# A fourth PSUM bank for the attention scores, and the epilogue's transposes in the bank of the product with the values

## The chip, the core and the metric

The kernel runs on one NeuronCore of one Trainium2 chip. The metric is device time of one execution in microseconds (us), as the median of several executions. The engines are named as the profile names them: PE is TensorE (PEld are its weight loads), DVE is VectorE, ACT is ScalarE, POOL is GpSimd, and SP is SyncE, which issues the DMAs. A line such as L1026 is a line of the kernel before.

## What is computed

One decoder layer over 2048 tokens of width 1024. After an RMSNorm and one input projection, half of the width goes through a gated DeltaNet (a chunked linear attention with a recurrent state), and the other half through a differential attention; an output projection brings both back to the residual stream. The change touches the differential attention, of which the core is:

```python
def block(args):                      # 128 queries against all earlier keys, 4 heads, 2 maps each
    q_blk, start = args
    s = jnp.einsum('bqhcd,bkhcd->bhcqk', q_blk, k).astype(jnp.float32)
    mask = key_pos[None, :] <= (start + jnp.arange(Q_BLOCK))[:, None]
    p = jax.nn.softmax(jnp.where(mask, s, neg), axis=-1)
    wts = p[:, :, 0] - lam * p[:, :, 1]
    return jnp.einsum('bhqk,bkhv->bqhv', wts.astype(v.dtype), v)
...
o = rmsnorm(o, out_gain) * (1.0 - lambda_init)
o = o * jax.nn.silu(z)                # then concatenated, and x + mixed @ w_out
```

## The kernel before, in words

Up to 1119 us of the profiled execution the kernel does the input projections and the DeltaNet. What follows is the attention, with the output projection mixed in between.

The attention works on 32 groups of 256 queries, in the order of the table SEQ: first the lower half of the sequence for the four heads (sixteen groups, with 2 to 8 blocks of 128 keys), then the upper half (sixteen groups, with 10 to 16 blocks). For each half group (qt is 0 or 1, 128 queries) three streams run side by side (`abreast`):

- `scores` (L1000): for each 512 keys and each of the two maps, PE writes a tile `sp` into a PSUM bank (two matmuls of 512 columns, and on the diagonal a third with the mask `cmask`), DVE takes the maximum `nm` (L1024), and ACT the exponential `ex` (L1026). The bank is free for a later tile when `ex` has ended.
- `values` (L1056) of the half group before: DVE joins the two maps (L1078), PE transposes the result into a bank `wtp`, ACT or DVE copies it to `wt`, and in the second half group PE accumulates `wt` times the values into one bank, `oT` (2g+2 products; each stands in the trace as two matmuls).
- `epilogue` (L1113) of the group before: ACT copies `oT` to `ob` (L1117), PE transposes it into `onp`, DVE clips it (`cl`, L1124), ACT squares it with a sum, DVE and POOL work out the norm (`aok`, `aso`, `afo`), DVE scales (`aon`, L1138), PE transposes it back into `aotp`, and DVE multiplies with the gate (`azz`, L847). ACT and POOL then split the result into two parts (`mxh`, `mxl`).

Beside these runs `behind`: the output projection, in blocks of twelve matmuls into a bank `outp` (L1260). As long as scores are left it has one bank of its own; after the last score, `obank` (L1210) deals blocks to the score banks as well. Its second half adds the residual, which is loaded ahead into two buffers, and stores the result.

The attention has eight PSUM banks: three for `sp`, two for `wtp`, one for `oT`, one named `ep` for `onp` and `aotp`, and one for `outp`. The program is written in the order of these streams. A list scheduler then sets the order on each engine: it takes an instruction when its own timeline says that the operands and the buffers are there. So the number of banks changes the order, and on the chip each engine keeps that order.

Of the kernel before, what the change touches and what calls it, by code (L numbers as in the profile page):

```python
# [16 lines left out]
P = 128  # L17
# [37 lines left out]
RATE_C = 5.0  # L55
KB = (2, 2)
LAGX = 5
SPB = 3
WTP = 2
EP = "ep"  # L60
EPB = 1
OTB = 1
LEADS = (0.0, 0.0, 0.0)
WOR = 2
EXB = 14
# [34 lines left out]
def hybrid_kernel(  # L100
# [36 lines left out]
    def mingle(a, b, rate, slack=0, drain=True):  # L137

        credit = 0.0
        steps = [None] * (slack + 1)  # L140
        done = object()
        while a or (b and drain):
            last[0] = None
            r = next(a, done) if a else "wait"
            if last[0]:
                steps = steps[1:] + last
            step = steps[0]
            credit = rate[0] if r else credit + rate[0]
            q = None
            while b and (credit > 0 or not a) and not q:  # L150
                with tc.issue_after(step.ins) if step else ExitStack():
                    q = next(b, done)
                credit -= 1.0
            assert not (r == "wait" and q == "wait"), "stuck"
            a = None if r is done else a
            b = None if q is done else b
        return b
# [20 lines left out]
    def bc(ap, shape):  # L178
        return ap.broadcast_to(shape)
# [665 lines left out]
    def mixed_out(src, gain, zz, g, c, pool, n, off, keep=False):  # L845
        hi, lo = (pool.tile([P, n], F32R, tag=t, name=t, bufs=MXB if pool is ap else 1) for t in ("mxh", "mxl"))
        V.scalar_tensor_tensor(zz, src, gain, zz, op0=ALU.mult, op1=ALU.mult)  # L847
        A.copy(hi, zz)
        PL.tensor_tensor(lo, zz, f(hi), op=ALU.subtract)
        if keep:  # L850
            return hi, lo
        for q, t in enumerate((hi, lo)):
            SY.dma_start(out=mx_d[g][0][q, c, :, off : off + n], in_=f(t))
# [105 lines left out]
    def bank(tag, name, bufs, shape=S4):  # L959
        return psa.tile(shape, F32, tag=tag, name=name, bufs=bufs)  # L960
# [4 lines left out]
    def turn():  # L965
        turns[0] += 1
        return turns[0] % 2
# [32 lines left out]
    def scores(c, qt):  # L1000
# [6 lines left out]
        for pi in range(npc):  # L1007
            k0 = pi * G
            w = min(G, n - k0)
            for m in range(2):  # L1010
                sp = bank("sp", "sp", SPB, [P, G])
                diag = pi == npc - 1
# [27 lines left out]
    def factors(c, qt, npc):  # L1040

        al, ss = c["al"], c["ss"]
        cf = ap.tile([P, 5], F32, tag="cf", name="cf", bufs=3)
        if npc > 1:
            st = ap.tile([P, 2], F32, tag="st", name="st", bufs=3)
            V.tensor_tensor(ss[:, :, :npc], ss[:, :, :npc], al[:, :, :npc], op=ALU.mult)
            V.tensor_reduce(st, ss[:, :, :npc], axis=AX.X, op=ALU.add)
        else:
            st = ss[:, :, 0]
        rs = c["rs"][:, qt, :]  # L1050
        V.reciprocal(rs, st)
        V.scalar_tensor_tensor(cf[:, 4:5], rs[:, 1:2], lv, st[:, 0:1], op0=ALU.mult, op1=ALU.mult)
        A.activation(cf[:, :npc], al[:, 1, :npc], AF.Copy, scale=cf[:, 4:5])  # L1053
        return cf

    def values(c, qt):  # L1056

        n = (2 * c["g"] + qt + 1) * P
        npc = (n + G - 1) // G
        nblk = 2 * c["g"] + 2  # L1060
        ex, al, wt = c["ex"], c["al"], c["wt"]
        ending = scored[0]
        c0, c = c, dict(c)
        for pi in range(npc):
            w = min(G, n - pi * G)
            nbk = w // P
            if pi not in wt:
                wt[pi] = ap.tile([P, 4, 2 * P], F32, tag="wt", name="wt", bufs=WTB)
            e0, e1 = ex[0, pi], ex[1, pi]
            if npc > 1:  # L1070
                if ending:
                    V.tensor_scalar(e0[:, :w], e0[:, :w], al[:, 0, pi : pi + 1], None, op0=ALU.mult)
                else:
                    PL.tensor_scalar(e0[:, :w], e0[:, :w], al[:, 0, pi : pi + 1], 1.0, op0=ALU.mult, op1=ALU.mult)  # L1074
            if pi == 0:
                yield
                cf = factors(c, qt, npc)
            V.scalar_tensor_tensor(e1[:, :w], e1[:, :w], cf[:, pi : pi + 1], e0[:, :w], op0=ALU.mult, op1=ALU.add)  # L1078
            tp = bank("wtp", "wtp", WTP)
            for j in range(nbk):  # L1080
                PE.transpose(tp[:, j, :], e1[:, j * P : (j + 1) * P], ident)
            wd_ = wt[pi][:, :nbk, qt * P : (qt + 1) * P]
            if turn():
                A.copy(wd_, tp[:, :nbk, :])  # L1084
            else:
                V.tensor_copy(wd_, tp[:, :nbk, :])
            yield
            if qt:
                if pi == 0:
                    oT = bank("oT", "oT", OTB).rearrange("p a b -> p (a b)")[:, : 2 * P]  # L1090
                else:
                    pv(c, oT, pi - 1, nblk)
                    yield
        if qt:
            pv(c, oT, npc - 1, nblk)
            yield
            c0["oT"] = oT

    def pv(c, oT, pi, nblk):
        for j in range(4 * pi, min(4 * pi + 4, nblk)):  # L1100
            c0 = P if j == nblk - 1 else 0
            PE.matmul(
                oT[:, c0:],
                lhsT=vv[c["h"], j // 8][:, j % 8, :],
                rhs=c["wt"][pi][:, j % 4, c0:],
                start=(j == 0),
                stop=(j == nblk - 1),
            )
# [4 lines left out]
    def epilogue(c):  # L1113
        oT = c["oT"]
        rs = c["rs"][:, :, 0]
        ob = ap.tile([P, 2 * P], F32, tag="ob", name="ob", bufs=1)
        A.mul(ob, oT, 2.0**-9)  # L1117
        onp = bank(EP, "onp", EPB)[:, :2]
        for qt in range(2):
            PE.transpose(onp[:, qt, :], ob[:, qt * P : (qt + 1) * P], ident)  # L1120

        S3 = [P, 2, P]
        cl = ap.tile(S3, F32, tag="cl", name="cl", bufs=1)
        V.tensor_scalar(cl, onp, 2.0**60, -(2.0**60), op0=ALU.min, op1=ALU.max)  # L1124
        so = ap.tile([P, 2], F32, tag="aso", name="aso", bufs=2)
        sq = ap.tile([P, 2], F32, tag="asq", name="asq", bufs=2)
        for qt in range(2):
            A.activation(cl[:, qt, :], cl[:, qt, :], AF.Square, scale=rs[:, qt : qt + 1], accum_out=sq[:, qt : qt + 1])
        yield
        ok = ap.tile([P, 2], F32, tag="aok", name="aok", bufs=2)  # L1130
        V.scalar_tensor_tensor(ok, sq, 2.0**88, rs, op0=ALU.is_lt, op1=ALU.mult)
        PL.tensor_scalar(so, sq, 2.0**87, 2.0**33, op0=ALU.min, op1=ALU.mult)
        PL.tensor_scalar(so, so, EPS, 1.0, op0=ALU.add, op1=ALU.mult)
        fo = ap.tile([P, 2], F32, tag="afo", name="afo", bufs=2)
        PL.tensor_tensor(fo, so, mhalf[:, :2], op=ALU.pow)
        V.tensor_tensor(fo, fo, ok, op=ALU.mult)
        on = ap.tile(S3, F32, tag="aon", name="aon", bufs=1)
        V.tensor_tensor(on, onp, bc(fo.unsqueeze(2), S3), op=ALU.mult)  # L1138
        yield
        otp = bank(EP, "aotp", EPB)  # L1140
        for qt in range(2):
            PE.transpose(otp[:, qt, :], on[:, qt, :], ident)
        g = c["g"]
        kept[g] = mixed_out(
            otp.rearrange("p a b -> p (a b)")[:, : 2 * P], dfg, c["zz"], g // 2, 4 + c["h"], ap, 2 * P, (g % 2) * 2 * P,
            c["h"] == SEQ[-1][0] and g in LASTG,
        )
        mixed[g] += 1
        yield
# [58 lines left out]
    spare = [0]  # L1208

    def obank():  # L1210

        spare[0] += scored[0]
        if spare[0] % 4:
            return bank("sp", "outp", SPB, [P, G])
        return pso.tile([P, G], F32, tag="outp", name="outp", bufs=1)

# [63 lines left out]
    def out_last(wo):  # L1280

        g = SEQ[-1][1]
        parts = []
        for tt in (2 * g, 2 * g + 1):
            mt = load_mixed(1, tt)
            for ch in range(2):
                xr = load_rest(tt, CS[ch], ap, ("ex", "ex"), EXB)
                o = obank()
                parts.append((ch, tt, xr, o))
                yield from share(1, tt, o, wo[ch], mt, HEADS[:-1])  # L1290
        while mixed[g] < H:
            yield "wait"
        for ch, tt, xr, o in parts:
            yield from share(1, tt, o, wo[ch], None, HEADS[-1:])
            result(tt, CS[ch], xr, o)
# [36 lines left out]
    b = mingle(gdn(), behind(), pace, SLACK, drain=False)  # L1332
# [34 lines left out]
```

## Time and profile before

| | us |
|---|---|
| median of 3 executions (1675.3 to 1682.5) | 1680.2 |
| the profiled execution | 1688.5 |
| its span in the trace | 1686.8 |
| busy of the span: PE / DVE / ACT / POOL | 1584.1 / 1067.4 / 788.4 / 697.7 |
| before the first score | 1119.2 |
| first score to last score | 516.3 |
| last score to the end of the span | 51.3 |

In the rows further below, "A <- B: 13.4, 19, 2.2" in a view of waits says that engine and line A sat idle for 13.4 us in total, in 19 places, at most 2.2 us at a time, until B ended. Matmuls are pipelined: the duration of one in the timeline includes what overlaps with the next, so the cost of one in a run of many is read from the chain of work, which counts each stretch of time once.

### The profile page before, as it was taken

The page shows a single profiled execution, that of the slowest core. Times are in us where ns is not written, and L with a number is a line of the kernel's source. Part 1 is how long each engine was busy: PE and PEld are TensorE (multiplying, and loading weights), DVE is VectorE, ACT ScalarE, POOL GpSimd, SP SyncE. Part 2 cuts the span into 40 slices and gives each one's busy share as a digit, 9 for nine tenths or more (in the row PEclk, how much of TensorE's full clock was granted, in tenths as well). Part 3 has the DMA queues.
Part 4 walks back from the last instruction along what each step waited for, and adds up shares of the span by engine and source line. Part 5 has one row for each costly group of instructions (what it writes and reads, how often), then busy time and mean ns, then how long its engine had stood idle before and what let it go on. Part 6 is the DMA issues. An engine that isn't in the chain of part 4 may idle for free.

```text
span 1686.8 us, 27350 instructions
## 1 busy us (share of the span) xinstructions
PE 1584.1 (94%) x9388; PEld 1374.7 (82%) x9388; DVE 1067.4 (63%) x2435; ACT 788.4 (47%) x2409; POOL 697.7 (41%) x846
## 2 busy tenths in 40 slices
PE   5999999999998999999999999889999989998997
PEld 4888898888987988898889898678778767777876
DVE  3765666746444684756654543338888768888872
ACT  4444444343345444334434343337777555565540
POOL 2464375352352347257442352213333353443343
PEclk8999999999999999999999999899999989999999
DMA  7342245233336432424422322896653364743344
GB/s 171 74 101 63 54 86 124 51 96 56 77 99 134 83 92 72 73 57 107 107 59 73 49 71 70 195 265 199 185 150 112 114 175 132 187 137 108 98 159 156
DMA packets 187703, 188.51 MB, mean 112 GB/s; under 512 B 12978, under 2 KB 143148, under 8 KB 187564
## 3 DMA queue, kind: packets, MB, share of 16 engines
q1 hardware_dynamic: 187564, 186.76, 43.6%
q8 instruction: 74, 1.21, 0.3%
q14 instruction: 65, 0.53, 0.1%
HBM read 124.82 MB, written 61.90 MB: 111 GB/s over the span
## 4 chain that ended last, share of the span: by engine, by line
PE 73%; DVE 10%; DMA 7%; ACT 3%; POOL 3%; issue 2%; SPq 1%; DVEq 0%; ACTq 0%; POOLq 0%
PE pct L130 25%; PE pnat L130 13%; PE outp L130 8%; PE oT L130 6%; PE sp L130 5%; PE wtp L133 2%; DVE nm L1024 2%; DMA u_gcr<-gc_d 2%; DMA wor<-in_w_out_dram 2%; DVE ex L1078 1%; PE gqp L130 1%; PE op L130 1%; PE ysp L130 1%; ACT ex L1026 1%; DVE qkraw L510 1%
## 5 line engine op out<-in xcount | busy, mean ns | idle before, releaser
L1026 ACT ACTIVATE ex<-sp,nm 128x512 f32<-128x512 f32 (+3 forms) x320 | 198.5, 625 | 100.2 <-DVE nm L1024 82.4
L130 PE MATMUL outp<-wo,mt 128*128 128x512 f32 x720 | 205.7, 416 | 10.8 <-ACT wo L1203 5.2
L1024 DVE TENSOR_REDUCE nm<-sp 128x1 f32<-128x512 f32 (+3 forms) x320 | 186.8, 602 | 26.4 <-PE sp L130 24.8
L130 PE MATMUL sp<-k,qs 128*128 128x512 f32 (+3 forms) x640 | 184.3, 393 | 19.0 <-ACT ex L1026 17.9
L130 PEld LDWEIGHTS outp<-wo,mt 128*128 128x128 f32 x720 | 130.2, 192 | 35.7 <-ACT wo L1203 5.9
L130 PE MATMUL pnat<-wh_fqk,xh 128*128 128x256 f32 (+1 forms) x512 | 152.9, 300 | 5.5 <-DVE xl L342 2.5
L130 PE MATMUL pnat<-wl_fqk,xh 128*128 128x256 f32 (+1 forms) x512 | 151.4, 297 | 1.3 <-POOL wl_fqk L361 1.3
L130 PE MATMUL pnat<-wh_fqk,xl 128*128 128x256 f32 (+1 forms) x512 | 150.5, 295 | 0.0
L130 PEld LDWEIGHTS sp<-k,qs 128*128 128x128 f32 x640 | 107.5, 191 | 47.9 <-ACT ex L1026 35.2
L1074 POOL TENSOR_SCALAR ex<-ex,al 128x512 f32<-128x512 f32 (+3 forms) x140 | 94.5, 691 | 95.6 <-ACT al L1035 92.3
L130 PE MATMUL oT<-wt,v 128*128 128x256 f32 (+1 forms) x576 | 132.6, 374 | 1.4 <-ACT wt L1084 1.4
L564 DVE SCALAR_TENSOR_TENSOR cy<-craw,cc,cy 128x512 f32<-128x512 f32 x144 | 124.0, 862 | 3.3
L130 PEld LDWEIGHTS oT<-wt,v 128*128 128x128 f32 x576 | 108.3, 193 | 17.7 <-ACT wt L1084 2.4
L1078 DVE SCALAR_TENSOR_TENSOR ex<-ex,cf 128x512 f32<-128x512 f32 (+3 forms) x160 | 111.2, 739 | 9.7 <-ACT cf L1053 9.2
L130 PEld LDWEIGHTS pnat<-wh_fqk,xh 128*128 128x128 f32 x512 | 100.7, 197 | 7.5 <-issue 2.6
L130 PE MATMUL pct<-xh,wh_dvz 128*128 128x512 f32 x256 | 104.1, 407 | 0.0
L130 PE MATMUL pct<-xl,wh_dvz 128*128 128x512 f32 x256 | 103.5, 404 | 0.0
L130 PE MATMUL pct<-xh,wl_dvz 128*128 128x512 f32 x256 | 103.5, 405 | 0.0
L130 PEld LDWEIGHTS pnat<-wl_fqk,xh 128*128 128x128 f32 x512 | 100.9, 197 | 2.3 <-POOL wl_fqk L361 1.7
L130 PE MATMUL pct<-xh,wh_dqk 128*128 128x512 f32 x256 | 102.3, 399 | 0.0
L130 PE MATMUL pct<-xl,wh_dqk 128*128 128x512 f32 x256 | 102.1, 399 | 0.0
L130 PEld LDWEIGHTS pnat<-wh_fqk,xl 128*128 128x128 f32 x512 | 100.9, 197 | 0.3
(280 smaller groups left out, 4132.4 us busy)
## 6 DMA issues: line engine op xcount, KB each, us to landing
qs<-qst_d SPq DMA_DIRECT2D x128, 128.0 KB, 3.8
mt<-mx_d SPq DMA_DIRECT2D x48, 256.0 KB, 4.8
k<-kst_d SPq DMA_DIRECT2D x40, 256.0 KB, 6.2
wr_dqk<-in_w_in_dram SPq DMA_DIRECT2D x32, 256.0 KB, 5.0
wr_dvz<-in_w_in_dram SPq DMA_DIRECT2D x32, 256.0 KB, 6.0
qst_d<-qkhl SPq DMA_DIRECT2D x16, 512.0 KB, 2.8
kst_d<-qkhl SPq DMA_DIRECT2D x16, 512.0 KB, 7.8
part_d<-xr SPq DMA_DIRECT2D x32, 256.0 KB, 4.1
```

What stands on the lines that cost most here:

```text
L130: last[0] = nc.tensor.matmul(*a, **k)
L133: last[0] = nc.tensor.transpose(*a, **k)
L510: V.tensor_tensor(rv, rv, bc(r[:, j].unsqueeze(2), [P, 4, 64]), op=ALU.mult)
L564: V.scalar_tensor_tensor(y, raw[:, j : j + G], convc[:, j, idx : idx + 1], y, op0=ALU.mult, op1=ALU.add)
L1024: V.tensor_reduce(mx, sp[:, :w], axis=AX.X, op=ALU.max, negate=True)
L1026: A.activation(e[:, :w], sp[:, :w], AF.Exp, bias=mx, accum_out=ss[:, m, pi : pi + 1])
L1074: PL.tensor_scalar(e0[:, :w], e0[:, :w], al[:, 0, pi : pi + 1], 1.0, op0=ALU.mult, op1=ALU.mult)
L1078: V.scalar_tensor_tensor(e1[:, :w], e1[:, :w], cf[:, pi : pi + 1], e0[:, :w], op0=ALU.mult, op1=ALU.add)
```

## The change

The tile pool for the scores gets four banks in place of three. The bank `ep` is gone: `onp` and `aotp` are taken from the tag `oT`, which keeps its one bank. `obank` now leaves out one block in five for its own bank, not one in four. The number of banks stays eight (4 + 2 + 1 + 1). No operation is added or taken away.

```diff
-SPB = 3
+SPB = 4
 WTP = 2
-EP = "ep"
-EPB = 1
-OTB = 1
@@ values
-                    oT = bank("oT", "oT", OTB).rearrange("p a b -> p (a b)")[:, : 2 * P]
+                    oT = bank("oT", "oT", 1).rearrange("p a b -> p (a b)")[:, : 2 * P]
@@ epilogue
         A.mul(ob, oT, 2.0**-9)
-        onp = bank(EP, "onp", EPB)[:, :2]
+        onp = bank("oT", "onp", 1)[:, :2]
...
-        otp = bank(EP, "aotp", EPB)
+        otp = bank("oT", "aotp", 1)
@@ obank
         spare[0] += scored[0]
-        if spare[0] % 4:
+        if spare[0] % (SPB + 1):
             return bank("sp", "outp", SPB, [P, G])
```

What this does to the order begins with the first scores; up to there every engine's order is the same, row for row. The line numbers after the change are smaller by three (L127 is the helper for matmuls, L1114 is `ob`, L1023 is `ex`).

On PE, in the group of head 1 with the last keys of the lower half (the eighth group), these rows stand from its `onp` on; `wo_...` are halves of the output weights, `v_13002` the values of the next head and here of the tenth group, `k_...` are keys. Before:

```order
L133 MATMUL onp<-ident,ob 128x128 x2
L130 MATMUL sp<-k_12996,qs 128x384 x2
L130 MATMUL sp<-cmask,identr 128x128
L133 MATMUL wtp<-ident,ex 128x128 x5
L130 MATMUL outp<-wo_11787,mt 128x512
L130 MATMUL outp<-wo_11788,mt 128x512
L130 MATMUL outp<-wo_11787,mt 128x512
L130 MATMUL oT<-wt,v_13002 128x256 x3
L130 MATMUL oT<-wt,v_13002 128x128
L130 MATMUL sp<-k_12999,qs 128x384 x2
L130 MATMUL sp<-cmask,identr 128x128
```

And after the change, where `v_12420` are the group's own values:

```order
L127 MATMUL oT<-wt,v_12420 128x256 x3
L127 MATMUL oT<-wt,v_12420 128x128
L130 MATMUL wtp<-ident,ex 128x128 x4
L127 MATMUL outp<-wo_11787,mt 128x512
L127 MATMUL outp<-wo_11788,mt 128x512
L127 MATMUL outp<-wo_11787,mt 128x512
L130 MATMUL wtp<-ident,ex 128x128 x2
L130 MATMUL onp<-ident,ob 128x128 x2
L130 MATMUL wtp<-ident,ex 128x128 x7
L127 MATMUL sp<-k_13575,qs 128x128 x2
L130 MATMUL aotp<-ident,aon 128x128 x2
```

Before, the product of a group two further on stands between `onp` and its `aotp` (which comes eight rows further on); after, both transposes come right behind the group's own product, and the next group's product follows behind `aotp`.

On ACT, around the `ob` of the fourteenth group, before:

```order
L1026 ACTIVATE ex,ss<-sp,nm 128x512 x2
L1035 ACTIVATE al<-al 128x2x2
L1026 ACTIVATE ex,ss<-sp,nm 128x512
L848 CAST mxh<-azz 128x256
L1026 ACTIVATE ex,ss<-sp,nm 128x128 x2
L1117 ACTIVATE ob<-oT 128x256
```

And after:

```order
L1274 COPY xr<-outp 128x512
L845 CAST mxh<-azz 128x256
L1032 ACTIVATE al<-al 128x2x3
L1114 ACTIVATE ob<-oT 128x256
L1125 ACTIVATE cl,asq<-cl,rs 128x128 x2
L1023 ACTIVATE ex,ss<-sp,nm 128x512 x2
```

Before, seven exponentials of tiles that PE scores only behind this group's last product stand ahead of its `ob`. After, `ob` and the squares stand ahead of the exponentials of four tiles that PE has scored already.

On PE, at the end of the program, before (from the last `aotp` on):

```order
L133 MATMUL aotp<-ident,aon 128x128 x2
L130 MATMUL outp<-wo_15583,mxh 128x512
L130 MATMUL outp<-wo_15584,mxh 128x512
L130 MATMUL outp<-wo_15623,mxh 128x512
L130 MATMUL outp<-wo_15624,mxh 128x512
```

And after:

```order
L130 MATMUL aotp<-ident,aon 128x128 x2
L127 MATMUL outp<-wo_15623,mt 128x512
L127 MATMUL outp<-wo_15624,mt 128x512
L127 MATMUL outp<-wo_15623,mt 128x512 x2
L127 MATMUL outp<-wo_15624,mt 128x512
L127 MATMUL outp<-wo_15623,mt 128x512 x2
```

Before, the twelve matmuls that need the last group's `mxh` and `mxl` follow right behind its `aotp`; after, thirty that don't need them come in between. In all, 168 output matmuls stand behind the last score after the change, and 108 before it.

## Rows read from the trace of the kernel before

**Rows 1.** The page, busy time of the engines and their share of the span.
```profile
PE 1584.1 (94%) x9388; PEld 1374.7 (82%) x9388; DVE 1067.4 (63%) x2435; ACT 788.4 (47%) x2409; POOL 697.7 (41%) x846
```

**Rows 2.** Stretches of the attention: lower half, upper half, end; busy us (instructions).
```profile
core 0: us, PE busy (x) PEld busy (x) DVE busy (x) ACT busy (x) POOL busy (x), PEclk, DMA share, GB/s
1119.00:1291.00 172.00, 164.60 (x920) 139.26 (x919) 142.97 (x433) 126.13 (x426) 55.34 (x98) 1.00 0.62 176
1291.00:1640.00 349.00, 323.85 (x1646) 263.23 (x1644) 281.17 (x632) 204.48 (x623) 144.79 (x198) 0.98 0.46 137
1640.00:1687.00 47.00, 35.74 (x150) 28.00 (x150) 15.03 (x30) 3.53 (x10) 13.64 (x13) 0.90 0.48 161
```

**Rows 3.** Waits of PE and its weight loads, 1291 to 1640 us.
```profile
PE sp L130 <- ACT ex L1026: 13.4, 19, 2.2
...
PE wtp L133 <- DVE ex L1078: 3.7, 4, 1.7
...
PEld sp L130 <- ACT ex L1026: 27.0, 42, 2.4
```

**Rows 4.** The page's groups: line, engine, operation, tile, count | busy, mean ns | idle before.
```profile
L1026 ACT ACTIVATE ex<-sp,nm 128x512 f32<-128x512 f32 (+3 forms) x320 | 198.5, 625 | 100.2 <-DVE nm L1024 82.4
...
L1024 DVE TENSOR_REDUCE nm<-sp 128x1 f32<-128x512 f32 (+3 forms) x320 | 186.8, 602 | 26.4 <-PE sp L130 24.8
```

**Rows 5.** Timeline of the thirteenth group (start us, us, instruction), lower half.
```profile
1245.59 0.87 PE L130 MATMUL oT<-wt,v 128*128 128x256 f32 x4
...
1254.69 0.39 ACT L1117 ACTIVATE ob<-oT 128x256 f32<-128x256 f32 x1
...
1255.89 1.73 PE L130 MATMUL oT<-wt,v 128*128 128x256 f32 x8
...
1275.67 0.47 DVE L847 SCALAR_TENSOR_TENSOR azz<-aotp,dfg,azz 128x256 f32<-128x256 f32 x1
```

**Rows 6.** Timeline of an epilogue in the upper half, from its last product on.
```profile
1533.28 0.81 PE L130 MATMUL oT<-wt,v 128*128 128x256 f32 x4
...
1534.41 0.37 ACT L1117 ACTIVATE ob<-oT 128x256 f32<-128x256 f32 x1
...
1535.80 0.39 PE L133 MATMUL onp<-ident,ob 128*128 128x128 f32 x2
...
1541.10 0.41 DVE L1138 TENSOR_TENSOR aon<-onp,afo 128x256 f32<-128x256 f32 x1
...
1542.70 0.47 DVE L847 SCALAR_TENSOR_TENSOR azz<-aotp,dfg,azz 128x256 f32<-128x256 f32 x1
```

**Rows 7.** The chain of work, last epilogue (start us, us, what), engines otherwise nearly idle.
```profile
1671.88 0.23 PE onp L133 x2
...
1676.12 0.49 DVE azz L847
```

**Rows 8.** The chain of work elsewhere: runs of matmuls, each stretch counted once.
```profile
1144.49 1.28 PE sp L130 x7
...
1145.99 2.74 PE outp L130 x12
...
1148.72 0.87 PE sp L130 x6
...
1422.75 0.88 PE wtp L133 x8
```

**Rows 9.** Waits of PE at the end, 1640 to 1687 us.
```profile
PE aotp L133 <- DVE aon L1138: 2.9, 2, 1.5
PE outp L130 <- DVE xr L1255: 1.8, 1, 1.8
PE outp L130 <- POOL mxl L849: 1.3, 1, 1.3
PE outp L130 <- ACT mxh L848: 1.1, 1, 1.1
```

## The prediction

> **What bounds the kernel now.** I read the page first, then the stretches of the attention, then the waits of PE in each, and last the timeline and the chain of work at the few places that the change touches. Up to the first score, at 1119 us, the order of every engine is the same before and after, so that part is taken over unchanged. In the page PE is busy for 94% of the span and DVE for 63% [rows 1]; in the attention PE is busy for 164.6 of 172 us in the lower half and for 323.9 of 349 us in the upper half [rows 2]. PE is therefore what bounds both, and the number of its matmuls doesn't change. What the change can win or lose is PE's waiting: 7.4 us in the lower half (172 - 164.6), 25.1 us in the upper half (349 - 323.9), and what it waits at the end. In the upper half most of it is one wait: PE wants to score a tile and all three banks still hold tiles that ACT hasn't finished. PE itself is idle for 13.4 us of that, in 19 places, and the weight loads are for 27.0 us, in 42 places [rows 3]; the loss lies between the two, since part of the idle time of the loads lies beside a matmul that still runs.
>
> **Term 1, the fourth bank.** PE may now be four tiles ahead of the exponentials, not three. One of the waits is 0.71 us long on average (13.4/19) and 2.2 us at most [rows 3]; a bank more is worth the time that the slower of the two readers takes for one tile, some 0.62 us [rows 4]. A single wait is then nearly covered. In a run of tiles the gain comes only once, since PE then meets the pace of DVE and ACT again. I take two thirds of the middle of both rows: 2/3 of (13.4 + 27.0)/2 = 13.5 us. The ends are 4 us (each run meets the same pace) and 22 us (nearly all). The lower half has such waits as well, but there they are counted within term 2.
>
> **Term 2, one bank for the product and the epilogue.** Before, the next group's product could start long before the epilogue of the last was through. In the lower half it always did: the thirteenth group's product ends at 1246.5 us, its copy `ob` starts at 1254.7, the next product starts at 1255.9, and its `azz` comes at 1275.7 [rows 5]. After, no product starts until the `azz` of the group before has ended, since `oT`, `onp` and `aotp` take turns in one bank. For each group PE thus has a chain to wait for (copy, transpose, norm, transpose, gate), and what hides it is only what stands between the last product of one group and the first of the next in PE's order.
>
> How long is the chain? In an epilogue of the upper half the product ends at 1534.1 and `azz` ends at 1543.2, which is 9.1 us; 1.0 us of it is PE's own work between the end of `ob` (1534.8) and `onp` (1535.8), and doesn't count [rows 6]. That leaves 8.1 us, with DVE and ACT about as busy as usual. The lower bound is the last epilogue of the program, when nothing else asks for the engines: 4.7 us from `onp` to the end of `azz` [rows 7], with 0.4 us for `ob` and a hop, 5.2 us. The upper bound is a copy or a DVE step that comes behind other work; in rows 5 `ob` alone came 8.2 us late. I don't take that, since in the new order `ob` stands ahead of the exponentials of tiles that are already scored, where before it stood behind seven of tiles that weren't; four exponentials ahead of it, 2.5 us by rows 4, make 10.6 us, which is my upper end.
>
> What hides it: between two products of the lower half the new order has, on average over the sixteen groups, 12.8 output matmuls, 20.0 matmuls of scores and masks, and 14.5 transposes. By the runs in the chain of work these take 0.228 (2.74/12), 0.165 ((1.28 + 0.87)/13) and 0.11 us (0.88/8) each [rows 8], so 2.9 + 3.3 + 1.6 = 7.8 us. The mean hides more than half of the groups, so I count them one by one, each score tile at its width: 16.0, 10.4, 10.5, 6.5, 7.8, 5.2, 7.6, 4.1, 7.3, 6.2, 7.0, 8.3, 6.5, 4.5, 8.5 and 7.3 us. Against 8.1 us, eleven of them fall short, by 19 us in sum (the eighth by 4.0, the fourteenth by 3.6, the sixth by 2.9); against 5.2 us the sum is 2, against 10.6 it is 51. While PE stands there, DVE and ACT catch up, so the 7.4 us that PE waits in this stretch today [rows 2] won't come on top: 19 - 7.4 = 11.6 us lost, with ends at -5 and +44. In the upper half the same sum between products is 10.4 to 14.9 us in every group, above the chain at 8.1 and nearly always at 10.6, so there the shared bank costs nothing; it would cost from about 10.4 us on.
>
> A rule of the Trainium skill speaks against this half of the change: Perfetto Trace Analysis, section Optimizing Tensor Performance, Matmuls, asks that independent groups of matmuls rotate through different banks, so that the evacuation of one overlaps the matmuls of the next. By that rule alone the lower half would lose the whole overlap, and the fourth score bank would win by the same sentence; it names no price, and what hides the chain is read from the order above.
>
> **Term 3, the end.** After the last score, 168 output matmuls are left (108 before), so PE has more to do while the last two epilogues run, and thirty matmuls stand between the last `aotp` and the twelve that need its result. The waits of PE in the last 47 us are 2.9 + 1.8 + 1.3 + 1.1 = 7.1 us [rows 9], and the granted clock there is 0.90 of full speed after them [rows 2]. I take both as mostly gone: 8 us won, with ends at 4 and 12. What PE does more at the end it does less before; that is no cost as long as the residual loads (two buffers) keep up.
>
> **The sum.** 1688.5 (the profiled execution, its span 1686.8 and 1.7 around it) + 11.6 - 13.5 - 8 = 1678.6 us, 0.59% less. The median of the runs shown is 1680.2, 8.3 us below the profiled execution; scaled by the same ratio it becomes 1670 us.
>
> **Rivals.** (a) *The chain is dearer than its cover* (slower). Place: the lower half, between a product and the next. DVE is busy for 143 of 172 us there [rows 2], and the chain crosses it five times, so each step may queue. At 10.6 us a group the shortfall is 51 us: 51 - 7.4 - 13.5 - 8 = +22, so 1702 us. It decides from a chain of about 8.9 us on, where the shortfall reaches the 28.9 us that the rest gives back. The rule named above would point here: groups that don't rotate lose their overlap. Against it stands that `ob` is early in the new order.
> (b) *The bank changes nothing* (no change). ACT waits 82.4 us for the maximum `nm` on DVE [rows 4], so what delays a bank is often DVE, at work on something else; PE would run one tile further ahead and then wait in the same way, or at `wtp` for DVE, as it does for 3.7 us now [rows 3]. Term 1 shrinks to 4 us: 11.6 - 4 - 8 = -0.4, so 1680 us. The fourth bank is used, in any case: the new order has up to four score tiles in a row.
> (c) *The chain is hidden nearly everywhere* (clearly faster). With `ob`, `cl` and the squares early, the chain comes near its bare 5.2 us. The shortfall is 2 us, the lower half wins some 3 us by the fourth bank as well: 2 - 3 - 13.5 - 8 = -22.5, so 1658 us.
>
> **How the numbers follow.** Chances: my forecast 0.36, (a) 0.22, (b) 0.22, (c) 0.20. The forecast is the likeliest, 1670 us. Half a per cent, 8.4 us, is about what a measurement of this kernel can tell from no change; the forecast lies just beyond it, so of its 0.36 I give 0.22 to faster, 0.13 to the same and 0.01 to slower. With (c) all faster, (b) 0.18 the same and 0.04 slower, and (a) 0.20 slower and 0.02 the same, it is 0.42 faster, 0.33 the same, 0.25 slower. The range leaves out the outer parts of (a) and of (c): 1652 to 1695 us.
>
> **What would show it.** Term 1: the wait of PE for `ex` in the upper half, 13.4 us, falls to 5 or less, and `wtp` doesn't take its place. Term 2: in the lower half PE waits at `onp`, `aotp` or the first `oT` for `ob`, `aon` or `azz`, 10 to 25 us in sum, and the time from a product's end to its `azz` falls from some 25 us to 8 or 9. Term 3: hardly a wait of PE behind the last score but for the last store, at full clock. I am wrong if the chain is still above 9 us in the lower half, if the upper half shows waits for `azz`, or if the clock falls in PE's new pauses, which would make each of them dearer than its length.

## The result, and the profile after the change

The changed kernel takes 1721.4 us (median of 4, 1714.6 to 1724.7), the kernel before 1681.4 us (median of 4): the ratio is 1.0228, with a 95% interval of 1.0204 to 1.0252. It is 2.3% slower. The prediction was 1670 us, with a range of 1652 to 1695. The profiled execution after the change took 1714.6 us, the lowest of its four, and its span is 1712.8 us.

The page's first part, busy time and share of the span, answers [rows 1]:

```profile
PE 1594.5 (93%) x9388; PEld 1379.2 (81%) x9388; DVE 1066.6 (62%) x2435; ACT 786.6 (46%) x2409; POOL 697.5 (41%) x846
```

No engine has more work. PE's share falls, so the time went into waiting. Where, is read from the stretches of the attention. I cut them at the same place of the program in every kernel: the lower half ends at the first product of the seventeenth group, the upper half at the last score. Before the change that is 1291.2 and 1635.5 us, after it 1343.0 and 1638.3 us. The columns are those of [rows 2]; after the change:

```profile
1114.00:1343.00 229.00, 198.17 (x1001) 157.53 (x999) 165.26 (x486) 141.74 (x473) 64.22 (x115) 0.96 0.50 144
1343.00:1638.00 295.00, 279.54 (x1438) 230.76 (x1438) 249.76 (x558) 181.78 (x561) 126.55 (x169) 0.98 0.45 136
1638.00:1712.80 74.80, 61.16 (x276) 49.65 (x274) 24.93 (x49) 8.93 (x26) 22.35 (x24) 0.95 0.51 168
```

In the lower half PE is idle for 30.8 of 229 us; before it was 7.4 of 172 [rows 2]. The lengths can't be compared directly, because the scheduler has also moved output matmuls between the stretches. So I use the **loss** of a stretch: for each matmul the time from the end of the one before it to its own end, less what one of its kind costs in an undisturbed run (0.231 us for `outp`, 0.216 for `oT` of 256 columns and half of that for 128, 0.109 for a transpose, 0.233 for a score of 512 columns, 0.17, 0.112 and 0.061 for 384, 256 and 128; within a few per cent of [rows 8]). This takes in idle time, late weight loads and what is lost at a lower granted clock, and leaves the moved work out. Each loss is read from the one profiled execution of a kernel:

| loss of PE, us | lower half | upper half | end | sum |
|---|---|---|---|---|
| before | 17.1 | 47.9 | 11.8 | 76.8 |
| after | 58.7 | 36.5 | 13.4 | 108.6 |
| difference | +41.6 | -11.4 | +1.6 | +31.8 |

The whole loss, and more, is in the lower half. The waits of PE there, before (1119 to 1291 us) and after (1114 to 1343 us): waiting line, what it waits for, us in total, times, longest.

```profile
PE sp L130 <- ACT ex L1026: 4.5, 12, 1.2
...
PE aotp L133 <- DVE cf L1052: 0.8, 1, 0.8
```

```profile
PE sp L127 <- ACT ex L1023: 19.1, 20, 2.4
PE aotp L130 <- DVE aon L1135: 5.7, 5, 1.7
PE oT L127 <- DVE azz L844: 1.7, 3, 1.0
```

Read by its names alone this looks like a lack of score banks: PE waits for exponentials four times as long as before, though it has a bank more, and only 1.7 us for the `azz` that releases the product's bank. The page says the same of the whole attention (idle before the groups of `sp`, and of `ex`; compare [rows 4]). The line of `sp` before, and then the lines after:

```profile
L130 PE MATMUL sp<-k,qs 128*128 128x512 f32 (+3 forms) x640 | 184.3, 393 | 19.0 <-ACT ex L1026 17.9
```

```profile
L1023 ACT ACTIVATE ex<-sp,nm 128x512 f32<-128x512 f32 (+3 forms) x320 | 198.1, 626 | 79.0 <-DVE nm L1021 48.6
...
L127 PE MATMUL sp<-k,qs 128*128 128x512 f32 (+3 forms) x640 | 182.9, 396 | 32.0 <-ACT ex L1023 30.4
L1021 DVE TENSOR_REDUCE nm<-sp 128x1 f32<-128x512 f32 (+3 forms) x320 | 183.4, 601 | 33.9 <-PE sp L127 33.2
```

The timeline of the eighth group (start, us, instruction) shows what stands behind that. It answers [rows 5]:

```profile
1228.78 0.60 PE L127 MATMUL oT<-wt,v 128*128 128x256 f32 x3
...
1229.47 0.39 ACT L1114 ACTIVATE ob<-oT 128x256 f32<-128x256 f32 x1 [0.73 <-PE oT L127]
...
1230.57 0.38 PE L130 MATMUL onp<-ident,ob 128*128 128x128 f32 x2
...
1231.62 0.40 ACT L1125 ACTIVATE cl<-cl,rs 128x128 f32<-128x128 f32 x1 [1.18 <-DVE cl L1121]
...
1232.53 0.16 DVE L1128 SCALAR_TENSOR_TENSOR aok<-asq,rs 128x2 f32<-128x2 f32 x1 [1.00 <-ACT cl L1125]
...
1233.18 0.71 POOL L1132 TENSOR_TENSOR afo<-aso,mhalf 128x2 f32<-128x2 f32 x1
1233.18 0.29 ACT L1050 ACTIVATE cf<-al,cf 128x1 f32<-128x1 f32 x1 [0.68 <-DVE cf L1049]
1233.38 0.67 ACT L1023 ACTIVATE ex<-sp,nm 128x512 f32<-128x512 f32 x1
...
1234.12 0.42 DVE L1135 TENSOR_TENSOR aon<-onp,afo 128x256 f32<-128x256 f32 x1
...
1234.19 0.44 PE L127 MATMUL sp<-k,qs 128*128 128x128 f32 x2 [2.40 <-ACT ex L1023]
...
1234.69 0.42 PE L130 MATMUL aotp<-ident,aon 128*128 128x128 f32 x2
...
1235.15 0.48 DVE L844 SCALAR_TENSOR_TENSOR azz<-aotp,dfg,azz 128x256 f32<-128x256 f32 x1
```

The product ends at 1229.4 and its `ob` follows at once, as forecast. Then ACT waits 1.18 us for DVE's clip, DVE 1.00 us for ACT's squares, and ACT another 0.68 us for DVE's factor `cf`, which stands behind the epilogue's `aok` in DVE's order. Four scored tiles stand behind all this in ACT's order; the first of their exponentials runs at 1233.38. PE comes to its next score early, finds all four banks full, and sits idle for 2.40 us; the epilogue's second transpose stands behind that score. The wait is booked on `ex`, but what made `ex` late is the chain of the epilogue, for which ACT and DVE stand still.

### The profile page after: what moved, and what is told of

It is laid out like the page before. It is cut to its first block, busy times and chain, and to the rows that moved or that the text cites. A ratio compares the mean times of both kernels' runs of the same rounds, so it can differ in the third digit from the quotient of the medians.

```text
span 1712.8 us, 27286 instructions
## 1 busy us (share of the span) xinstructions
PE 1594.5 (93%) x9388; PEld 1379.2 (81%) x9388; DVE 1066.6 (62%) x2435; ACT 786.6 (46%) x2409; POOL 697.5 (41%) x846
## 4 chain that ended last, share of the span: by engine, by line
PE 69%; DVE 13%; DMA 8%; ACT 4%; POOL 3%; issue 3%; SPq 1%; DVEq 0%; ACTq 0%; POOLq 0%
PE pct L127 25%; PE pnat L127 13%; PE outp L127 7%; PE oT L127 5%; PE sp L127 4%; DVE nm L1021 3%; DVE ex L1075 3%; DMA u_gcr<-gc_d 2%; ACT ex L1023 2%; PE wtp L130 1%; DMA wor<-in_w_out_dram 1%; PE gqp L127 1%; PE ysp L127 1%; PE op L127 1%; DVE qkraw L507 1%
## 5 line engine op out<-in xcount | busy, mean ns | idle before, releaser
L1023 ACT ACTIVATE ex<-sp,nm 128x512 f32<-128x512 f32 (+3 forms) x320 | 198.1, 626 | 79.0 <-DVE nm L1021 48.6
L127 PE MATMUL outp<-wo,mt 128*128 128x512 f32 x720 | 211.6, 428 | 18.4 <-DVE xr L1252 6.1
L127 PE MATMUL sp<-k,qs 128*128 128x512 f32 (+3 forms) x640 | 182.9, 396 | 32.0 <-ACT ex L1023 30.4
L127 PEld LDWEIGHTS outp<-wo,mt 128*128 128x128 f32 x720 | 136.2, 199 | 48.1 <-DVE xr L1252 7.1
L127 PEld LDWEIGHTS sp<-k,qs 128*128 128x128 f32 x640 | 107.0, 193 | 64.0 <-ACT ex L1023 52.7
L127 PE MATMUL pnat<-wh_fqk,xh 128*128 128x256 f32 (+1 forms) x512 | 152.3, 299 | 5.4 <-DVE xl L339 2.6
L127 PE MATMUL pnat<-wl_fqk,xh 128*128 128x256 f32 (+1 forms) x512 | 150.3, 295 | 0.8 <-POOL wl_fqk L358 0.8
L127 PE MATMUL pnat<-wh_fqk,xl 128*128 128x256 f32 (+1 forms) x512 | 149.6, 293 | 0.0
L127 PE MATMUL oT<-wt,v 128*128 128x256 f32 (+1 forms) x576 | 133.2, 381 | 2.2 <-DVE azz L844 2.2
L127 PEld LDWEIGHTS oT<-wt,v 128*128 128x128 f32 x576 | 112.4, 197 | 21.0 <-DVE azz L844 3.7
L1075 DVE SCALAR_TENSOR_TENSOR ex<-ex,cf 128x512 f32<-128x512 f32 (+3 forms) x160 | 114.7, 764 | 12.8 <-ACT cf L1050 7.7
L127 PEld LDWEIGHTS pnat<-wh_fqk,xh 128*128 128x128 f32 x512 | 99.9, 196 | 7.4 <-issue 3.0
L127 PE MATMUL pct<-xh,wh_dvz 128*128 128x512 f32 x256 | 103.4, 404 | 0.0
L127 PE MATMUL pct<-xl,wh_dvz 128*128 128x512 f32 x256 | 103.0, 402 | 0.0
L127 PE MATMUL pct<-xh,wl_dvz 128*128 128x512 f32 x256 | 102.7, 402 | 0.0
L127 PE MATMUL pct<-xh,wh_dqk 128*128 128x512 f32 x256 | 102.3, 399 | 0.0
L127 PE MATMUL pct<-xl,wh_dqk 128*128 128x512 f32 x256 | 102.1, 399 | 0.0
L127 PEld LDWEIGHTS pnat<-wl_fqk,xh 128*128 128x128 f32 x512 | 100.2, 196 | 1.8 <-POOL wl_fqk L358 1.3
L127 PE MATMUL pct<-xh,wl_dqk 128*128 128x512 f32 x256 | 101.0, 398 | 0.0
```

Of the source, the lines that this page charges most:

```text
L127: last[0] = nc.tensor.matmul(*a, **k)
L1023: A.activation(e[:, :w], sp[:, :w], AF.Exp, bias=mx, accum_out=ss[:, m, pi : pi + 1])
```

## The experiments

**Theory S** (sharing): in the lower half the time from a group's product to the next is set by the epilogue's chain, since product and epilogue take turns in one bank. **Rival F** (the fourth bank): the waits for `ex` are what they seem; the order that four banks bring runs scores ahead. Later **rival O**: the scheduler simply found a bad order for shared banks, whatever the chain's length. All ratios are against the kernel before on the same chip. Where two changed kernels are compared in us they may have run on different chips; the median of the kernel before was 1679.4 to 1682.8 us on all of them.

### 1. Sharing alone

```diff
-SPB = 4
+SPB = 3
```

This is the changed kernel without the fourth bank.

> The changed kernel with three score banks again: the product and the epilogue's two transposes take turns in one bank, and nothing else of the change is left (seven banks are used). Theory S (sharing): the chain from a group's product over the norm to `azz` stands in front of the next product, and the in-order queues of ACT and DVE pass that on to tiles that are already scored; the loss of 41 us comes from it alone. Then 1715 to 1735 us: no fourth bank gives back what little it gave. PE's loss in the lower half over its bare work stays near 61 us, as in the changed kernel (17 before). Rival F (the fourth bank): the order that four banks bring puts scores ahead of the rest, and PE waits for exponentials. Then 1675 to 1695 us, and the waits of `sp` for `ex` in the lower half fall back towards 9 us.

Measured: 1728.5 us (1726.6 to 1738.0), ratio 1.0288 (1.0247 to 1.0330). The losses are 59.5, 48.7 and 10.2 us. Against before that is +42 us in the lower half, +1 in the upper and -2 at the end. Theory S holds and F falls: the waits for `ex` in the lower half are the same with three banks.

```profile
PE sp L127 <- ACT ex L1023: 19.3, 22, 3.5
PE aotp L130 <- DVE aon L1135: 3.5, 3, 1.8
```

The fourth bank is worth the difference to the changed kernel: 7 us between the medians, 12 us of loss in the upper half between the two profiled executions.

### 2 to 4. Other banks for the epilogue

The kernel before with four score banks and the epilogue's transposes in the banks of `wtp`:

```diff
-SPB = 3
+SPB = 4
-EP = "ep"
-EPB = 1
+EP = "wtp"
+EPB = 2
```

> The kernel before with four score banks, and `onp` and `aotp` in the two banks of `wtp`; the product `oT` keeps a bank that no one else uses. Eight banks. Theory S: the next product no longer waits for the epilogue, only `wtp` has two more tiles a group to take in, so 1665 to 1690 us, and the lower half loses some 17 to 25 us of PE's time over its bare work. Rival F: the fourth bank is still there, so 1705 to 1725 us.

Measured: 1756.9 us (1753.9 to 1763.4), ratio 1.0455 (1.0410 to 1.0500); losses 64.6, 63.7 and 17.4 us. Both expectations missed: it is slower than sharing alone, although no other tile uses the product's bank. The waits of PE in the lower half have another name now:

```profile
PE aotp L133 <- DVE aon L1138: 14.2, 9, 2.6
PE sp L130 <- ACT ex L1026: 12.0, 14, 2.3
```

The kernel before, with product and epilogue taking turns in two banks:

```diff
-EP = "ep"
-EPB = 1
-OTB = 1
+EP = "oT"
+EPB = 2
+OTB = 2
```

> The kernel before with three score banks, and the product and the epilogue's transposes taking turns in two banks (as many as before, but not divided into one for each). Theory S: a second bank lets the next product start while the epilogue of the last is in its norm, so 1672 to 1695 us. Rival F: three score banks as before, so 1675 to 1690 us; this run doesn't tell the two apart by itself, but says what one bank more is worth to the sharing.

Measured: 1710.9 us (1706.9 to 1711.6), ratio 1.0167 (1.0135 to 1.0199); losses 40.3, 48.9 and 14.5 us. It is slower than either expectation. With two banks in turn, `oT`, `onp` and `aotp` alternate: the next product gets the bank of this group's `onp`, and so waits for `aon`, not for `azz`. Two banks, as many as before, cost 23 us of loss in the lower half, only because they are taken in turns. Theory S held in kind here, but I had put the loss too low.

The changed kernel with `aotp` alone in the banks of `wtp`:

```diff
-        otp = bank("oT", "aotp", 1)
+        otp = bank("wtp", "aotp", WTP)
```

> The changed kernel with `aotp` in the banks of `wtp`: the bank of the product is then given back when `aon` has read `onp`, some 2 us (0.6 for the transposes and a hop, 0.9 to 1.5 for `azz`) earlier than by `azz`. Theory S: shorter by up to 16 x 2 = 32 us in the lower half, of which some lies beside other work: 1690 to 1708 us. Rival F: 1712 to 1725 us.

Measured: 1780.3 us (1778.2 to 1784.6), ratio 1.0588 (1.0553 to 1.0623); losses 78.8, 74.4 and 21.9 us. A clear miss: the product's bank is free earlier, and the kernel is 59 us slower than the changed one. In the lower half:

```profile
PE aotp L130 <- DVE aon L1135: 24.6, 10, 3.9
PE sp L127 <- ACT ex L1023: 21.3, 10, 4.3
```

The order on PE says why. Banks of a tag are handed out in the order in which the program asks for them, so an `aotp` among the `wtp` tiles keeps every later `wtp` behind it. Between `onp` and `aotp`, while the norm runs, PE has on average 8.1 transposes of `wtp` in the lower half before the change and 6.3 after it; here it has none, in all sixteen groups (in experiment 2, where `onp` is among them as well, 4.4 on average). So the theory is wider than I had it: whatever takes turns with the epilogue stands still for its norm, be it the product or the transposes.

### 5 and 6. The chain without the norm

The same steps on the same engines, but `aon` is scaled by a factor that is there early, so that the output is left without its norm; in the changed kernel and in the kernel before:

```diff
-        V.tensor_tensor(on, onp, bc(fo.unsqueeze(2), S3), op=ALU.mult)
+        V.tensor_tensor(on, onp, bc(rs.unsqueeze(2), S3), op=ALU.mult)
```

> The changed kernel with `aon` scaled by `rs`, which is there early, in place of `fo`: the norm's steps are all still done, but nothing waits for their result, so that the output isn't normalised. The chain from the product to `azz` loses the 4 to 5 us from `cl` to `fo`, at equal work on every engine. Theory S (the length of the chain against its cover): the lower half's loss over PE's bare work falls from 59 us to 15 to 30, so 1680 to 1695 us. Rival O (the order that the scheduler makes when one bank is taken in turns, whatever the chain's length): 1708 to 1722 us.

> The same edit on the kernel before, as a control (its output isn't normalised either). There no product waits for the norm. Theory S: 1668 to 1682 us. Rival O: the same; if this falls as far as the run on the changed kernel, the norm's wait costs wherever it stands, and theory S falls.

Measured: with the shared bank 1664.3 us (1662.2 to 1666.5), ratio 0.9896 (0.9864 to 0.9928), losses 13.7, 34.7 and 7.2 us; with the banks of before 1689.8 us (1683.4 to 1694.1), ratio 1.0045 (1.0025 to 1.0066), losses 13.1, 50.0 and 19.1 us. The same edit takes 57 us from the changed kernel, more than expected, and nothing from the kernel before, which ends above what I expected and loses 7 us more at the end. Rival O falls: with the short chain, the shared bank costs nothing, and the waits for `ex` are gone as well, though no score bank was added. The lower half of the first one, its stretch and its waits:

```profile
1114.00:1297.00 183.00, 179.69 (x999) 151.21 (x999) 162.61 (x483) 138.60 (x474) 65.61 (x111) 1.00 0.64 177
```

```profile
PE sp L127 <- ACT ex L1023: 1.9, 6, 0.7
```

### 7. The epilogue written first

```diff
-LEADS = (0.0, 0.0, 0.0)
+LEADS = (0.0, 0.0, 1.0)
```

> The changed kernel with the epilogue's three steps written ahead of the scores and the values that run beside it, so that the scheduler takes them first. Theory S: `ob` was prompt already (0.42 us behind the product), so the chain can only lose what its later steps wait in queues, 1 to 3 us a group: 1695 to 1718 us. Rival O: another order, as bad: 1715 to 1730 us.

Measured: 1724.8 us (1722.6 to 1727.8), ratio 1.0256 (1.0223 to 1.0290); losses 63.0, 39.3 and 17.4 us. Not faster than the changed kernel: it lies where rival O had it, not theory S. The median time from product to `azz` did fall, from 10.7 to 9.4 us, though the mean hardly did (10.1 and 10.0 us), and the loss of the lower half didn't fall. So the length of the chain alone doesn't set the loss; how that goes with theory S is told below under term 2, where the chain is taken apart.

### 8. Only `onp` shared

```diff
-        onp = bank(EP, "onp", EPB)[:, :2]
+        onp = bank("oT", "onp", OTB)[:, :2]
```

> The kernel before with `onp` in the bank of the product, and `aotp` alone in the bank `ep`; three score banks. The product's bank is free when `aon` has read `onp`, 7.5 to 8 us behind the product's end, not 10.2 us as with all three in one bank (1728 us). Theory S: the loss in the lower half falls from 59.5 to some 35 to 45 us, as with two banks taken in turns (40 us, 1711 us), so 1703 to 1715 us. Rival O: 1720 to 1730 us if the turn is what counts, about 1680 us if `aotp` was the costly part.

Measured: 1709.8 us (1704.9 to 1713.2), ratio 1.0164 (1.0128 to 1.0200); losses 36.8, 48.2 and 16.0 us, as theory S had it. With experiments 1 and 5 it gives three lengths of the bank's turn, with losses of 59.5 us (up to `azz`), 36.8 us (up to `aon`) and 13.7 us (no norm; four score banks).

### 9 and 10. The norm beside the bank's turn

The squares go to `ob`, so that `cl` stays as a copy of `onp` in SBUF, and the bank needn't wait for the norm. In the lower half, a group's `aotp` is written behind the `onp` of the next:

```diff
-            A.activation(cl[:, qt, :], cl[:, qt, :], AF.Square, ...)
+            A.activation(ob[:, qt * P : (qt + 1) * P], cl[:, qt, :], AF.Square, ...)
+        if late:
+            back(*late.pop())
...
-        V.tensor_tensor(on, onp, bc(fo.unsqueeze(2), S3), op=ALU.mult)
+        V.tensor_tensor(on, cl, bc(fo.unsqueeze(2), S3), op=ALU.mult)
         yield
+        if c["g"] < 4:
+            late.append((c, on))
+        else:
+            back(c, on)
```

`back` is the third step of the epilogue as it was; `aon` has two buffers and `azz` one more. Once on the banks of the changed kernel, once on those of before:

> The changed kernel (four score banks, product and epilogue in one bank) with the norm taken out of the bank's turn in the lower half: `aon` is scaled from `cl`, the clipped copy of `onp` in SBUF (the squares go to `ob` instead), and each group's `aotp` and gate are written behind the `onp` of the next group, when its `aon` has long been ready. What is computed is the same. Theory S: the bank's turn is product, `ob`, `onp`, `cl`, the `aotp` of the group before, `azz`, without the norm's 4 to 5 us, as in the run without the norm (1664 us, lower loss 13.7 us); so 1658 to 1675 us, lower loss 10 to 20 us. Rival O (that run was fast for its order or its data): 1690 to 1720 us.

> The same edit on the banks of before (three for scores, `onp` and `aotp` in a bank of their own). Theory S: no product waits for the norm there, so the edit has nothing to win: 1670 to 1692 us, lower loss 13 to 20 us (17 before). If this falls to 1665 us as well, the edit is a gain of its own, and the fourth bank's part is the difference.

Measured: 1675.3 us (1669.6 to 1679.4, 12 runs), ratio 0.9957 (0.9937 to 0.9976), losses 18.5, 31.1 and 12.0 us; and on the banks of before 1681.7 us (1679.2 to 1684.7), ratio 0.9998 (0.9987 to 1.0010), losses 16.3, 46.2 and 14.3 us. With the real norm the loss of the lower half falls from 58.7 to 18.5 us, and the time by 46 us. It ends at the upper edge of what I expected of it. The lower half of experiment 9, its stretch and its longest wait of PE:

```profile
1119.00:1301.00 182.00, 174.74 (x972) 147.19 (x971) 161.74 (x476) 135.29 (x463) 64.09 (x110) 1.00 0.59 169
```

```profile
PE sp L127 <- ACT ex L1023: 4.4, 8, 1.4
```

The edit by itself wins nothing, and the same edit on the new banks ends 6 us lower (15 us of loss in the upper half): that is again the fourth bank.

### 11 and 12. Four residual buffers

```diff
-                xr = load_rest(tt, CS[ch], op_, ("xr", "xq"), 2)
+                xr = load_rest(tt, CS[ch], op_, ("xr", "xq"), 4)
...
-                xr = op_.tile([P, G], F32, tag="xr", name="xr", bufs=2)
+                xr = op_.tile([P, G], F32, tag="xr", name="xr", bufs=4)
```

On the kernel of experiment 9, and on the changed kernel alone:

> The kernel with the norm aside, and four residual buffers in place of two. If the loss behind the last score is the loads of the residual, which wait for the store from the same buffer, 4 to 8 us less than with the norm aside alone: 1652 to 1668 us. If it is not, the same as that run within 2 us.

> The changed kernel with four residual buffers in place of two, and nothing else. Theory R (the missing gain at the end is the residual's loads): the loss behind the last score falls from 13.4 us to 5 to 9 us, the time to 1711 to 1718 us. Rival: the epilogues of the last two groups hold PE there: 1719 to 1724 us.

Measured: 1665.3 us (1660.8 to 1669.0, 6 runs), ratio 0.9892 (0.9870 to 0.9915), losses 19.9, 31.3 and 5.2 us; alone 1708.7 us (1707.7 to 1710.3), ratio 1.0156 (1.0134 to 1.0178), losses 62.3, 30.2 and 10.1 us. In the first pair the medians differ by 10 us, a little more than expected, and the loss falls at the end alone, by 6.8 us: the residual's loads held it, as theory R said. In the second the medians differ by 13 us, more than expected, and only 3 us of loss is gone at the end, less than expected. PE's wait there for `xr` falls from 6.1 to 2.5 us, but a wait of 3.4 us for `aon` comes in its place, as the rival had it. Another 6 us of loss is gone in the upper half, where output blocks run too, and 4 us are added in the lower half; why, I haven't followed further.

The kernel of experiment 11 does the whole computation, and is 1.1% faster than the kernel before and 3.3% faster than the changed one (1665.3 / 1721.4 = 0.967). Four residual buffers on the kernel before were not tried, so how much of the 1.1% needs the new banks is open.

## Why the prediction was wrong, point by point

**Term 1, the fourth bank: right in size and place, in part by luck.** I took 13.5 us in the upper half, with ends at 4 and 22. The loss there fell by 11.4 us between the two profiled executions, by 12.2 us against sharing alone and by 15.1 us between experiments 10 and 9; the medians of these two pairs differ by 7 and 6 us. But the gain was to come from the wait for `ex`, 13.4 us in [rows 3], which was to fall to 5. It is still this, between 1343 and 1638 us:

```profile
PE sp L127 <- ACT ex L1023: 11.3, 12, 3.3
PE wtp L130 <- DVE wt L1083: 1.5, 2, 1.0
```

The loss at the scores fell only from 28.8 to 24.5 us, which is my lower end of 4. What went besides is the late `wtp`, whose loss fell from 15.1 to 3.4 us. In the two pairs that differ by the bank alone (1 and the changed kernel, 10 and 9), the scores, `wtp` and `aotp` each lose 3 to 5 us less. How a score bank helps the other two isn't shown. Rival (b) said that PE would go on to wait for `ex` in the same way, and that was so; that it would wait at `wtp` instead was not.

**Term 2, the shared bank: this step failed.** I had +11.6 us, ends -5 and +44; the runs show +42. The place was right: of the 58.7 us of the lower half, 56 us lie between a group's product and the next group's first one, and there the next product does come right behind `azz` (0.6 us, the median). In the upper half, where I expected no cost, sharing alone added 0.8 us of loss. The cover was also counted rightly, group for group (16.0, 10.4, 10.5, 6.5, 7.8, 5.2 us ... in the trace), except that it holds the chain's own four transposes, 0.4 us a group; without them the shortfall against 8.1 us is 24 us, not 19.

Wrong was to set the whole cover against the whole chain. PE keeps its order, so a matmul hides only that part of the chain beside which it stands. Over the sixteen groups after the change, by the trace, each part from the end of one matmul to the end of another, with the cost of each kind as in the loss:

| part of the chain | it took, us | PE's work in it, us | loss, us |
|---|---|---|---|
| last product to first `onp` | 35.4 | 32.9 | 2.5 |
| first `onp` to first `aotp` (the norm) | 102.1 | 65.4 | 36.7 |
| first `aotp` to the next product | 46.2 | 28.9 | 17.3 |

The norm takes 6.4 us a group, and stands beside 4.1 us of PE's work. In the eighth group, five `outp` stand behind `aotp`, where only `azz` was left to hide. Added up as one, these covers look nearly enough; each group loses 3.5 us on average, and the five whose cover was longer than the 8.1 us that I took lose 0.5, 2.5, 1.9, 5.2 and 5.5 us, where I had nothing. The rows that I had could have told it: the three parts of the chain in [rows 6], 0.7 us up to the end of `ob`, 5.7 us from `onp` to the end of `aon` and 1.7 us from there to the end of `azz`, fall short by 1, 30 and 7 us against the cover of each part by itself, 38 us in sum and not 24. Experiment 7 fits this. There PE's work beside the norm is 54.6 us and that behind `aotp` 39.2 us; the norm's part loses 44.8 us and the last part 11.7 us, so that the sum doesn't fall. No run moves PE's work towards the norm and leaves the chain as it is, so whether a better order could hide it is open.

The chain's own length was nearly right. From product to `azz` it took 10.1 us on average, of which 1.3 us lie between the end of `ob` and `onp`, which I had left out; that leaves 8.7 us, where I took 8.1. But `onp` to the end of `aon` took from 3.8 to 8.5 us, by the group, and why it varies so I haven't followed. The 18 us between 38 and the measured 56 hold that and the lower clock (see the last section), and I can't divide them. My upper end of 10.6 us a group comes out at +44, close to the measured value; since the chain was not that long and the cover was set against it in the wrong way, that agreement is chance. So rival (a) was the right one, for a reason it didn't have. I had let a prompt `ob` speak against it. `ob` was prompt (it ended 0.42 us behind the product, the median), but it is the shortest part of the chain.

**What the waits looked like.** I expected PE to wait at `onp`, `aotp` or the first `oT` for 10 to 25 us. It waits 8 us there (0.7 at `onp`, 5.7 at `aotp`, 1.7 at `oT`), and 19 us at `sp` for `ex`. ACT and DVE take their instructions in order too: while they wait for a step of the chain, ready exponentials stand behind it, as in the timeline of the eighth group. Experiment 5 shows that this wait belongs to the chain. Of the signs of being wrong that I named, all three are there: 10.1 us from product to `azz`, a granted clock of 0.96 in the lower half, and a little of the third, 1.0 us of waits for `azz` in the upper half.

**The rule I weighed.** The Trainium skill (Perfetto Trace Analysis, section Optimizing Tensor Performance, Matmuls) asks that independent groups of matmuls rotate through different banks. It pointed to rival (a), and the runs agree with it for the chain as it is (42 us of loss in the lower half). Experiment 9 marks the limit: groups in one bank cost nothing measurable (a lower loss of 18.5 us against 16.3 with a bank apart) when the long step has been taken out of the bank's turn.

**Term 3, the end: wrong by 10 us.** I took 8 us won; the loss went from 11.8 to 13.4 us. The waits for `aon` and for `mxh` and `mxl` in [rows 9] are gone, as I said. The condition that I named in a half-sentence, that two residual buffers keep up, did not hold. PE at the end, 1638 to 1713 us, and a piece of the chain of work there:

```profile
PE outp L127 <- DVE xr L1252: 6.1, 4, 3.5
PE outp L127 <- DMA mt<-mx_d: 2.9, 1, 2.9
```

```profile
1661.01 3.17 DMA out_dram<-xr
1664.20 2.57 DMA xr<-in_x_dram
...
1666.93 1.27 POOL xr L1248
...
1668.22 0.70 DVE xr L1252
...
1668.97 4.36 PE outp L127 x12
```

A result is stored, the buffer is loaded again with the next residual, POOL and DVE add, and only then is the bank free in which PE puts its next block: 8 us around one buffer. With four buffers the wait of PE for `xr` is 1.8 us (experiment 11), and the loss at the end 5.2 us.

**The sum.** By the losses +41.6 - 11.4 + 1.6 = +31.8 us; between the two profiled executions it is 1714.6 - 1688.5 = 26.1 us, since the changed one was also 5.4 us earlier at its first score, where nothing differs. The medians are 40 us apart.

## What to carry to other kernels

In this kernel, a buffer that two steps share cost what lies between its first write and its last read, and of the bound engine's work only what stood in order beside each part of that hid it. So split the chain at the engine's own instructions, and set cover against length part by part. The engine's wait may then be booked on a neighbour (here the exponentials), because every in-order queue in the chain stands still for it; shortening the chain at equal work told the two apart. Before a bank is given to someone else, take the long step out of its turn (a copy to SBUF, a later second half), and look at the next buffer in line, here two residual buffers at the end.

## What the runs showed of the hardware

A pause of PE can cost more than its length. In the lower half the granted clock was 1.00 before [rows 2], and 1.00 in experiment 5. It was 0.96 with the shared bank, 0.95 in experiment 1 and 0.91 in experiment 4, where PE waits longer. Four-microsecond stretches around the pause shown above (columns as in [rows 2]):

```profile
1220.00:1224.00 4.00, 1.66 (x7) 0.66 (x5) 3.97 (x13) 1.75 (x6) 0.44 (x1) 1.00 0.36 114
1224.00:1228.00 4.00, 3.95 (x19) 3.31 (x20) 1.58 (x3) 0.74 (x2) 0.73 (x1) 1.00 0.22 75
1228.00:1232.00 4.00, 3.80 (x26) 3.15 (x24) 1.05 (x3) 2.09 (x6) 0.00 (x0) 1.00 0.89 262
1232.00:1236.00 4.00, 1.81 (x8) 1.56 (x9) 2.73 (x12) 3.32 (x13) 1.14 (x3) 0.87 0.40 111
1236.00:1240.00 4.00, 4.00 (x17) 3.38 (x17) 1.36 (x6) 2.49 (x10) 1.79 (x3) 0.70 0.29 95
1240.00:1244.00 4.00, 4.00 (x26) 3.41 (x26) 3.37 (x11) 3.64 (x12) 0.28 (x2) 1.00 0.33 106
```

From 1232 us on PE is busy for 1.81 of 4 us, and in the next four, in which it is busy throughout, 0.70 of full speed is granted, a mixture of 1.2 and 2.4 GHz; then it is 1.00 again. Not every pause has this: between 1220 and 1224 us PE was busy for 1.66 us, and the clock stayed at 1.00 there and in the next stretches. An estimate from the clock of the stretch: 0.04 of 229 us is 9 us of cycles not granted in the lower half, of which some fell into idle time; so up to 9 of the 42 us are the clock's, and are within the loss as I measure it.

How closely a loss repeats can be read from experiments 9 and 11, whose lower and upper halves differ by 1.4 and 0.2 us; the changed kernel and experiment 12 differ by 3.6 us in the lower half. So one difference of a few us of loss, taken alone, should not be read as an effect.
